# The opening of a two-block kernel: tensor-engine work in a written order, row tiles loaded ahead of weights, modulation sums in blocks of eight, six PSUM banks

## The chip, the cores and the metric

The kernel runs on one core of a Trainium2 chip. The metric is the time of one execution on the device, in microseconds (us). The engines are named by their columns in the profile: PE is the tensor engine (TensorE), PEld its weight loads, DVE is VectorE, ACT is ScalarE, POOL is GpSimd, SP is SyncE, which here issues the DMAs.

## The reference, cut to what matters

Two model blocks run one after the other on 512 rows of 1024 features, all in fp32. The first block has two layers of a mixer and an MLP. The part that matters is the beginning of layer 0:

```python
c_act = silu(c)                                     # one vector of 1024
mod = c_act @ w_ada[0] + b_ada[0]                   # 1024 x 6144, split in six
sh_mix, sc_mix, ... = split(mod, 6)
h = rms_norm(x, g_pre_mix) * (1 + sc_mix) + sh_mix  # 512 x 1024
u = h @ w_in                                        # 1024 x 4096
x_m, z, glu_a, glu_b = split(u, [1024, 2048, 3072])
x_c = silu(causal_depthwise_conv(x_m, 4 taps))      # -> q, k ; x_m -> v
a = glu_a * sigmoid(glu_b)
a = silu(group_layer_norm(causal_depthwise_conv(a, 31 taps)))
y = concat([sigmoid(z) * h_m, a]) @ w_out           # h_m: the mLSTM of q, k, v
x = x + gt_mix * rms_norm(y, g_post_mix)
```

So nothing of `u` can be computed before `sh_mix` and `sc_mix` are there, and these need 2048 columns of `w_ada`, 8 MB.

## The kernel before, in words

**Products.** Each fp32 operand is split into a high part in fp32r and a low part (the rest). A product is three matmuls, high by high, high by low and low by high: `mm3`, lines 163 to 166. ScalarE makes the high part by a cast, and the low part is a subtraction (`sub`, line 143) on VectorE or on GpSimd (argument `P`). Weights pass through three raw buffers (`wrp`), four buffers of high parts (`whp`) and four of low parts (`wlp`). Larger SBUF tiles come from a list of 35 slots (`A`, `free`).

**PSUM.** There are eight banks of 128x512: four for main products (`mm`), two long banks (`long_bank`) in which the 31 taps of the depthwise convolution are accumulated by VectorE, and two for transposes (`tr`).

**The opening.** It has four stages, p = 0 to 3, one for each pair of 128-feature tiles. `stage(p)` (line 1295) runs `ada_first(p)` (line 428): eight loads of 256 KB of `w_ada`, and one matmul for each of the eight contraction tiles, 128x512 with the vector `c` replicated to 32 columns, in four column groups of the array (`tile_position=(0, 32 * g)`, line 439). Their sums lie in a long bank. ScalarE copies them (line 444), TensorE transposes them (line 447), and VectorE reduces and adds (lines 449, 450) and scales (line 391). Then `stage` loads 512 columns of `w_in` (two of the gated unit's column blocks), casts and subtracts them, and `mix[0].turn` transposes the normalised rows (line 218), applies scale and shift on ScalarE (line 224) and splits the result on VectorE (lines 231 and 143). In stage 0 the first two row tiles are loaded between the first loads of `w_ada`, the other two behind them; `post(t)` normalises a row tile (`xnorm`, `row_rstd`: lines 195 to 205). `proj_start` (line 258) holds four banks and, once the next stage has been written down, adds this stage's share to each: 24 matmuls a stage, 96 in all. Its consumer, `glu_cons(0)`, gates the result and starts `taps(0)`.

**After the opening.** Three further groups of the gated unit (`projA`, 96 matmuls each), then four projections of x (`xproj(h)`, 48 matmuls each, with the consumer `xm_cons`: a copy, a split and a convolution of four taps, which read the PSUM bank), q, k and v, the gates, z, the mLSTM, the convolution groups' norms (`conv_norm`, `conv_gate`, `conv_split`), and the projection by `w_out` (`projB_chunk`, and `projB_tail`, whose last two contraction tiles are those of the last convolution group).

**What sets the order.** SyncE's instructions are issued in the order in which the program writes them (`tc.manual_schedule(engines={SP})`). For the other engines a planner fixes the order when the kernel is built: it takes, engine by engine, what by its own cost model is ready, the earliest written first; `tc.high_priority(offset=-LOWP)` sets the taps 4000 places behind. Each engine then works through its own list in that order. Background work (`pending`, for example `ada_pair`) advances by one step with each weight unit that `wunit` loads.

## Time and profile before

Three runs took 2287.65, 2289.1 and 2289.36 us; the median is 2289.1.

| | before |
|---|---|
| profiled execution | 2287.21 us |
| its span, first to last instruction | 2285.2 us |
| PE busy | 98% of the span |
| DVE busy | 67% |
| ACT busy | 43% |
| POOL busy | 13% |
| DMA, mean over the span | 122 GB/s |
| mean granted clock of PE | 0.994 of 2.4 GHz |

A share of busy time is a mean over stages with different limits, so the stretches are read one by one. A matmul's listed duration overlaps the next one's; the pace is the distance from start to start.

### The profile page before, as it was taken

What the parts mean: (1) busy time and instruction counts of PE and PEld (TensorE: products, weight loads), DVE (VectorE), ACT (ScalarE), POOL (GpSimd) and SP (SyncE); (2) the same over time, 40 slices, a digit from 0 to 9 for tenths busy, and PEclk for the clock granted to TensorE, in tenths of its full rate; (3) what the DMA queues carried; (4) which work ended last, traced back from release to release, by engine and by line L of the source; (5) the groups of instructions that cost most, each with busy time, mean ns of one, the idle gap of its engine ahead of it and who ended that gap; (6) DMA issues with size and microseconds to landing.
All of it is one profiled execution on the core that took longest, in us unless ns stands there. A gap on an engine that the chain in (4) does not pass through costs nothing.

```text
span 2285.2 us, 29859 instructions
## 1 busy us (share of the span) xinstructions
PE 2240.0 (98%) x11164; PEld 1807.5 (79%) x11164; DVE 1530.7 (67%) x3037; ACT 979.1 (43%) x1651; POOL 301.3 (13%) x263
## 2 busy tenths in 40 slices
PE   8999999999999999999999999999999999999998
PEld 3777677878777888767887778888888888878886
DVE  4898998874555678899887643387566574652345
ACT  3557554543323334666543332235545554222232
POOL 1763000000000144400000000000321311000000
PEclk9999999999999999999999999999999999999999
DMA  7632134366565232321436544523211321532331
GB/s 265 211 116 79 55 120 131 128 198 194 179 190 176 87 117 85 92 65 47 148 120 187 177 127 127 170 75 114 88 50 54 98 77 60 172 95 94 99 131 65
DMA packets 194585, 277.69 MB, mean 122 GB/s; under 512 B 13812, under 2 KB 146548, under 8 KB 194440
## 3 DMA queue, kind: packets, MB, share of 16 engines
q1 hardware_dynamic: 194440, 275.78, 37.8%
q8 instruction: 88, 1.44, 0.3%
q14 instruction: 57, 0.47, 0.1%
HBM read 263.68 MB, written 14.37 MB: 122 GB/s over the span
## 4 chain that ended last, share of the span: by engine, by line
PE 74%; DVE 5%; ACT 2%; issue 1%; DMA 0%; POOL 0%; SPq 0%; DVEq 0%; ACTq 0%; POOLq 0%
PE mm L166 22%; PE mm L165 22%; PE mm L164 22%; PE cv L1129 1%; PE tr L1114 1%; PE mm L827 1%; PE mm L851 1%; PE mm L1093 0%; PE mm L1095 0%; DVE h L143 0%; PE tr L218 0%; DVE nt L176 0%; ACT sb L1103 0%; DVE h L231 0%; ACT junk L195 0%
## 5 line engine op out<-in xcount | busy, mean ns | idle before, releaser
L164 PE MATMUL mm<-h,wh 128*128 128x512 f32 (+1 forms) x1728 | 656.8, 381 | 3.8 <-DVE h L231 2.9
L165 PE MATMUL mm<-h,wh 128*128 128x512 f32 (+1 forms) x1728 | 654.3, 379 | 0.7 <-DVE h L143 0.6
L166 PE MATMUL mm<-h,wl 128*128 128x512 f32 (+1 forms) x1728 | 654.4, 379 | 0.1
L155 ACT CAST wh<-wr 128x1024 fp32r<-128x1024 f32 (+1 forms) x318 | 323.3, 1018 | 532.4 <-PE mm L165 249.7
L143 DVE TENSOR_TENSOR wl<-wr,wh 128x1024 fp32r<-128x1024 f32 x254 | 314.0, 1240 | 224.4 <-ACT wh L155 223.4
L164 PEld LDWEIGHTS mm<-h,wh 128*128 128x128 f32 x1728 | 324.7, 188 | 75.2 <-DVE h L231 6.8
L166 PEld LDWEIGHTS mm<-h,wl 128*128 128x128 f32 x1728 | 324.8, 188 | 68.3 <-issue 5.9
L165 PEld LDWEIGHTS mm<-h,wh 128*128 128x128 f32 x1728 | 325.3, 188 | 66.1 <-issue 3.0
L589 DVE SCALAR_TENSOR_TENSOR cv<-glu,vec,cv 128x511 f32<-128x511 f32 (+24 forms) x480 | 327.8, 732 | 7.1 <-ACT cv L584 6.8
L362 DVE SCALAR_TENSOR_TENSOR acc<-wr,csil,acc 128x1024 f32<-128x1024 f32 x91 | 116.1, 1284 | 127.6 <-DMA wr<-in_w_ada_dram 88.4
L165 PE MATMUL mm<-wl,hid 128*128 128x512 f32 x416 | 164.2, 395 | 0.0
L166 PE MATMUL mm<-wh,hid 128*128 128x512 f32 x416 | 164.1, 395 | 0.0
L164 PE MATMUL mm<-wh,hid 128*128 128x512 f32 x416 | 163.4, 395 | 0.0
L143 POOL TENSOR_TENSOR wl<-wr,wh 128x1024 fp32r<-128x1024 f32 (+1 forms) x68 | 137.8, 2033 | 185.0 <-ACT wh L155 144.4
L413 POOL PARTITION_BROADCAST G<-row x5 | 8.3, 1665 | 699.5 <-DVE row L410 383.4
L164 PEld LDWEIGHTS mm<-wh,hid 128*128 128x128 f32 x416 | 78.2, 188 | 19.9 <-issue 0.8
L166 PEld LDWEIGHTS mm<-wh,hid 128*128 128x128 f32 x416 | 78.2, 188 | 18.4
L165 PEld LDWEIGHTS mm<-wl,hid 128*128 128x128 f32 x416 | 78.2, 188 | 18.2
L543 ACT ACTIVATE s<-mm 128x512 f32<-128x512 f32 x64 | 38.0, 594 | 111.3 <-PE mm L166 111.3
L1103 ACT ACTIVATE sb<-sb,nm 128x512 f32<-128x512 f32 x64 | 46.4, 725 | 59.1 <-DVE nm L1101 50.2
L1083 POOL TENSOR_TENSOR bias<-band,amask 128x256 f32<-128x256 f32 x48 | 43.3, 910 | 206.5 <-DVE mx L1098 131.1
L546 DVE CAST hid<-s 128x512 fp32r<-128x512 f32 x64 | 29.0, 457 | 45.9 <-ACT s L544 45.9
(318 smaller groups left out, 3659.4 us busy)
## 6 DMA issues: line engine op xcount, KB each, us to landing
wr<-in_w_in_dram SPq DMA_DIRECT2D x140, 512.0 KB
wr<-in_w_ff_dram SPq DMA_DIRECT2D x128, 512.0 KB
wr<-in_w_ada_dram SPq DMA_DIRECT2D x80, 512.0 KB
wr<-in_w_out_dram SPq DMA_DIRECT2D x32, 512.0 KB
wr<-in_w_mod_dram SPq DMA_DIRECT2D x24, 512.0 KB
wr<-in_w_ada_dram SPq DMA_DIRECT2D x32, 256.0 KB
xd<-x SPq DMA_DIRECT2D x16, 512.0 KB
x<-xd SPq DMA_DIRECT2D x16, 512.0 KB
```

The lines of the kernel that those rows point to most:

```text
L143: (eng or V).tensor_tensor(dst, x_, h.bitcast(F32), op=ALU.subtract)
L155: S.copy(h, raw)
L164: PE.matmul(ps, ah, bh, start=first, stop=False)
L165: PE.matmul(ps, ah, bl, start=False, stop=False)
L166: PE.matmul(ps, al, bh, start=False, stop=last)
L362: V.scalar_tensor_tensor(acc, raw, cv[:, kt:kt + 1], acc, op0=ALU.mult, op1=ALU.add)
L543: act(s, ps[m], AF.Relu)
L546: V.tensor_copy(o[:, 0], s)
L589: V.scalar_tensor_tensor(pa[m][:, s:], at[:, m, :512 - s], vv("wdw", l * 248 + (2 * g + m) * 31 + j, 1), pa[m][:, s:], op0=ALU.mult, op1=A ...
L827: PE.matmul(ps[:, :n], k[h][:, kt, j * 128:j * 128 + 128], q[h][:, kt, j * 128:], start=kt == 0, stop=kt == 1)
L1083: P.tensor_tensor(btile[:, b].rearrange("p (c r) -> p c r", r=8), bands[i][:, hh, :, o:o + 32].rearrange("p r c -> p c r"), amask[:, var, ...
L1103: act(sb, sb, AF.Exp, bias=nm, accum_out=sm)
```

## The change

- In `stage(0)` all four row tiles are loaded first, then the weights.
- `ada_first` is cut in three: `ada_load` (eight loads), `ada_sums` (the eight matmuls, one behind the other, in a transposing bank instead of a long bank, and the copy) and `ada_cols` (the rest).
- A stage also loads 256 columns of `w_in` for the first projection of x (half a unit), in a raw buffer of its own, and casts and subtracts it. `stage` is now a generator in four steps: loads; sums; columns, casts and subtractions; transposes of the rows.
- `proj_start` holds six banks, the four main ones and the two long ones, and adds 36 matmuls a stage. Within it TensorE's order is the written one: this stage's banks 0 to 2, the next stage's sums, bank 3, its columns, bank 4, its row transposes, bank 5.
- Its consumers are `glu_cons(0)` and then `xm_cons(0)`; `xproj(0)` is left out of layer 0's later list.
- The second part of the vector table is loaded in stage 1 ahead of that stage's casts.

```diff
-    def proj_start(stage, hT, consumer):
-
-        ps = [mm() for _ in range(4)]
-        cur = stage(0)
-        for p in range(4):
-            if p < 3:
-                nxt = stage(p + 1)
-            h, lo = cur
-            for i in range(4):
-                for k in range(2):
-                    kt, w = 2 * p + k, 2 * (i // 2) + k
-                    c = slice((i % 2) * 128, (i % 2) * 128 + 128)
-                    mm3(ps[i], h[:, w, c], lo[:, w, c], hT[kt][:, 0], hT[kt][:, 1], kt == 0, kt == 7)
-            cur = nxt
-        consumer(ps)
+    def proj_start(lead, hT, consumers):
+
+
+        ps = [mm() for _ in range(4)] + [long_bank() for _ in range(2)]
+        with tc.manual_schedule(engines={mybir.EngineType.PE}):
+            cur = lead(0)
+            for _ in range(4):
+                w = next(cur)
+            for p in range(4):
+                nxt = lead(p + 1) if p < 3 else None
+                if nxt:
+                    next(nxt)
+                for i in range(6):
+                    h, lo = w[i // 4]
+                    for k in range(2):
+                        kt, q = 2 * p + k, 2 * ((i % 4) // 2) + k
+                        c = slice((i % 2) * 128, (i % 2) * 128 + 128)
+                        mm3(ps[i], h[:, q, c], lo[:, q, c], hT[kt][:, 0], hT[kt][:, 1], kt == 0, kt == 7)
+                    if nxt and i in (2, 3, 4):
+                        w_next = next(nxt)
+                if nxt:
+                    w = w_next
+        for k, f in enumerate(consumers):
+            f(ps[4 * k:4 * k + 4])
...
-    def ada_first(p):
-
-
-        ps = long_bank()
+    def ada_load(p):
         wv = wada[0][:, :, 0:2048].rearrange("p k (g n) -> p k g n", g=2)[:, :, :, p * 256:p * 256 + 256]
+        raws = []
         for kt in range(0, 8, 2):
             raw = A([128, 2, 2, 256], F32, "wr")
             for k in range(2):
                 SP.dma_start(raw[:, k], wv[:, kt + k])
-            for k in range(2):
-                g = (kt + k) % 4
-                PE.matmul(ps[32 * g:32 * g + 32, :], crep[:, kt + k], raw[:, k].rearrange("p g n -> p (g n)"),
-                          start=kt < 4, stop=kt >= 4, tile_position=(0, 32 * g))
-            free(raw)
-            yield
+            raws.append(raw)
+        return raws
+
+    def ada_sums(raws):
+
+
+        ps = tr()
+        for kt in range(8):
+            g = kt % 4
+            PE.matmul(ps[32 * g:32 * g + 32, :], crep[:, kt], raws[kt // 2][:, kt % 2].rearrange("p g n -> p (g n)"),
+                      start=kt < 4, stop=kt >= 4, tile_position=(0, 32 * g))
+        free(*raws)
         rows = t2([128, 512], F32, "rows")
         S.copy(rows, ps)
+        return rows
+
+    def ada_cols(p, rows):
         ps = tr()
...
         if l == 0:
-            proj_start(units, hT, glu_cons(0))
+            proj_start(units, hT, (glu_cons(0), xm_cons(0)))
...
-        xproj(0)
+        if l > 0:
+            xproj(0)
         xproj(1)
...
     def stage(p):
 
-        lead = ada_first(p)
         if p == 0:
-            for t in range(2):
-                next(lead)
-                load_x(t)
+            load_x(0, 1, 2, 3)
+        raws = ada_load(p)
+        w = []
+        for cols in ((2048, 3072), (0,)):
+            raw = wrp.tile([128, 2 * len(cols), 256], F32, tag="wr", name="wr")
+            for i, c0 in enumerate(cols):
+                SP.dma_start(raw[:, 2 * i:2 * i + 2], wi_[0][:, 2 * p:2 * p + 2, c0:c0 + 256])
+            w.append(raw)
+        if p == 1:
+            SP.dma_start(vec[:, NLEAD:], I["vec"][:, NLEAD:])
+        if p == 0:
+            for t in range(4):
                 mix[0].post(t)
-        for _ in lead:
-            pass
-        if p == 0:
-            for t in range(2, 4):
-                load_x(t)
-                mix[0].post(t)
-        raw = wrp.tile([128, 4, 256], F32, tag="wr", name="wr")
-        for i, c0 in enumerate((2048, 3072)):
-            SP.dma_start(raw[:, 2 * i:2 * i + 2], wi_[0][:, 2 * p:2 * p + 2, c0:c0 + 256])
-        h = whp.tile([128, 4, 256], F32R, tag="wh", name="wh")
-        lo = wlp.tile([128, 4, 256], F32R, tag="wl", name="wl")
-        S.copy(h, raw)
-        sub(lo, raw, h, P)
+        yield
+        rows = ada_sums(raws)
+        yield
+        ada_cols(p, rows)
+        for u, raw in enumerate(w):
+            n = raw.shape[1]
+            h = whp.tile([128, n, 256], F32R, tag="wh", name="wh")
+            lo = wlp.tile([128, n, 256], F32R, tag="wl", name="wl")
+            S.copy(h, raw)
+            sub(lo, raw, h, P)
+            w[u] = h, lo
+        yield
         for half in range(2):
             mix[0].turn(half, (p,))
...
-        return h, lo
+        yield w
```

## Rows read from the trace of the kernel before

**Rows 1.** The page's engine table: busy us, share of the span, instructions.

```profile
PE 2240.0 (98%) x11164; PEld 1807.5 (79%) x11164; DVE 1530.7 (67%) x3037; ACT 979.1 (43%) x1651; POOL 301.3 (13%) x263
```

**Rows 2.** Windows by stage: stretch, its length, busy us, clock, DMA share, GB/s.

```profile
core 0: us, PE busy (x) PEld busy (x) DVE busy (x) ACT busy (x) POOL busy (x), PEclk, DMA share, GB/s
0.00:26.68 26.68, 15.71 (x41) 3.43 (x41) 14.49 (x60) 10.09 (x24) 3.19 (x8) 0.87 0.97 329
67.49:367.87 300.38, 295.94 (x1332) 230.44 (x1331) 279.78 (x568) 167.29 (x293) 99.93 (x68) 0.99 0.38 122
```

**Rows 3.** Timeline of PE in the opening: start, us, instruction [idle before <-releaser].

```profile
26.68 1.22 PE L164 MATMUL mm<-h,wh 128*128 128x512 f32 x2
...
37.66 1.06 PE L439 MATMUL cv<-wr,crep 128*32 128x512 f32 x8
...
39.62 1.05 PE L439 MATMUL cv<-wr,crep 128*32 128x512 f32 x4
...
41.51 1.05 PE L439 MATMUL cv<-wr,crep 128*32 128x512 f32 x2
...
45.39 0.60 PE L447 MATMUL tr<-ident,rows 128*128 128x128 f32 x4
...
46.67 0.47 PE L164 MATMUL mm<-h,wh 128*128 128x512 f32 x1
...
49.63 1.91 PE L439 MATMUL cv<-wr,crep 128*32 128x512 f32 x12
...
61.35 0.51 PE L164 MATMUL mm<-h,wh 128*128 128x512 f32 x1 [0.31 <-DVE h L231]
...
62.36 0.40 PE L166 MATMUL mm<-h,wl 128*128 128x512 f32 x1
...
67.49 0.39 PE L164 MATMUL mm<-h,wh 128*128 128x512 f32 x1
```

**Rows 4.** Windows of 10 us through the opening.

```profile
0.00:10.00 10.00, 5.11 (x8) 0.73 (x8) 1.95 (x13) 2.84 (x6) 0.82 (x7) 1.00 0.78 250
10.00:20.00 10.00, 6.21 (x26) 2.01 (x25) 7.72 (x31) 6.23 (x16) 1.47 (x1) 0.99 1.08 382
20.00:30.00 10.00, 7.71 (x18) 2.04 (x13) 5.15 (x18) 1.02 (x2) 0.90 (x1) 0.50 1.09 361
30.00:40.00 10.00, 9.97 (x47) 5.67 (x48) 5.79 (x19) 3.46 (x6) 2.39 (x1) 1.00 1.10 368
```

**Rows 5.** Timeline of ACT, DVE and POOL in stages 0 and 3.

```profile
14.02 0.58 ACT L444 COPY rows<-cv 128x512 f32<-128x512 f32 x1 [2.56 <-PE cv L439]
...
15.62 0.16 DVE L450 TENSOR_TENSOR mf<-mf,vec 128x4 f32<-128x4 f32 x1
...
55.15 0.59 ACT L444 COPY rows<-cv 128x512 f32<-128x512 f32 x1 [4.38 <-PE cv L439]
...
56.76 2.40 POOL L143 TENSOR_TENSOR wl<-wr,wh 128x1024 fp32r<-128x1024 f32 x1 [8.25 <-ACT wh L1314]
56.86 2.32 DVE L450 TENSOR_TENSOR mf<-mf,vec 128x4 f32<-128x4 f32 x1
```

**Rows 6.** DVE: groups by line from 62 to 368 us, then the first taps.

```profile
L589 DVE SCALAR_TENSOR_TENSOR cv<-glu,vec,cv 128x511 f32<-128x511 f32 (+24 forms) x240 | 164.3, 732 | 3.8 <-ACT cv L584 3.6
...
L636 DVE SCALAR_TENSOR_TENSOR cv<-mm,vec,cv 128x511 f32<-128x511 f32 (+2 forms) x24 | 17.9, 745 | 0.2 <-ACT cv L633 0.2
...
69.18 7.04 DVE L589 SCALAR_TENSOR_TENSOR cv<-glu,vec,cv 128x511 f32<-128x511 f32 x10
```

**Rows 7.** Timeline of DVE: two of its waits in layer 0's mixer.

```profile
109.95 0.69 DVE L602 SCALAR_TENSOR_TENSOR glu<-th,mm 128x512 f32<-128x512 f32 x1 [2.24 <-ACT th L601]
...
192.49 0.49 DVE L700 BATCH_NORM_STATS2 bs<-cacc 128x6 f32<-128x128 f32 x2 [2.63 <-ACT cacc L697]
```

**Rows 8.** PE at the mixer's closing projection: timeline, then a window.

```profile
389.85 0.79 PE L164 MATMUL mm<-wha,cg 128*128 128x512 f32 x1 [2.11 <-ACT cg L730]
...
390.00:392.00 2.00, 2.00 (x5) 1.23 (x6) 1.97 (x4) 0.81 (x2) 0.00 (x0) 0.50 0.00 0
```

More of the change, by code (lines that the diff above doesn't have):

```diff
@@ L605, in glu_cons @@
             return f
-        if l == 0:
-            proj_start(units, hT, glu_cons(0))
-        else:
-            proj_first(units, hT, lambda: pre.turn(1), glu_cons(0))
-        for g in range(1, 4):
-            projA(wi, [2048 + 256 * g, 3072 + 256 * g], hT, glu_cons(g), eng=None if l == 0 and g == 2 else P)
-        free(glu[0])
-        if l == 0:
-            load_const()
-            free(crep)
         q, k, vf, v1, tz, xmh, xch = {}, {}, {}, {}, {}, {}, {}
-        wg = A([128, 4, 6, 32], F32, "wg")
-        SP.dma_start(wg, I["wg"][l])
         def xm_cons(h):
@@ L645, in xm_cons @@
             return fn
+        if l == 0:
+            proj_start(units, hT, (glu_cons(0), xm_cons(0)))
+        else:
+            proj_first(units, hT, lambda: pre.turn(1), glu_cons(0))
+        for g in range(1, 4):
+            projA(wi, [2048 + 256 * g, 3072 + 256 * g], hT, glu_cons(g), eng=None if l == 0 and g == 2 else P)
+        free(glu[0])
+        if l == 0:
+            load_const()
+            free(crep)
+        wg = A([128, 4, 6, 32], F32, "wg")
+        SP.dma_start(wg, I["wg"][l])
         def xproj(h):
@@ L1318, in stage @@
         if p == 1:
-            SP.dma_start(vec[:, NLEAD:], I["vec"][:, NLEAD:])
             for nm in ("wcm", "bcm", "gmh", "wdw", "gcn", "bcn", "wc2", "bc2"):
                 V.tensor_scalar(vv(nm), vv(nm), 0.5, None, op0=ALU.mult)
-        return h, lo
+        yield w
     mix[0].hT = [HL(512, f"h{f}") for f in range(8)]
```

## The prediction, as recorded before the changed kernel was run

> **What bounds the kernel now.** I read the page's engine table first: TensorE is busy for 2240.0 of 2285.2 us [rows 1], so a change pays only where TensorE waits, runs at the lower clock, or does the same sums in more time. The windows by stage then show where that is. In the first 26.68 us it has only 15.71 us of work, while the DMA engines are full at 329 GB/s [rows 2]; from 67.49 to 367.87 it has 295.94 of 300.38. The third view is its timeline through the opening [rows 3]. The first of the 96 main products (24 in each of four stages) starts at 26.68 and the next group of the projection starts at 67.49. The fourth is granted clock and DMA rate in steps of 10 us [rows 4]: clock 0.50 (the 1.2 GHz level) from 20 to 30, after gaps in TensorE's work, then full.
>
> A second bound lies behind the first. From 67.49 to 367.87 VectorE is busy for 279.78 of 300.38 us [rows 2], mostly with the 240 depthwise-convolution taps of this layer, 0.73 us each [rows 6]. At 389.85 TensorE waits 2.11 us for the last convolution group's output [rows 8]. The end of that chain, not only TensorE, decides when layer 0's mixer ends. So I reckon two sums: TensorE's lead at the end of the opening, and what VectorE's chain lets through.
>
> **Start of the main products.** All four row tiles now load ahead of the modulation weights. From the rates of [rows 4], 2.50 MB have landed by 10 us, 6.32 by 20, 9.93 by 30. Before, the last weights of the first sum stood behind 3.23 MB (0.08 of vectors, 2.10 of weights, 1.05 of rows), at 11.9 us, and the copy of its result began at 14.02 [rows 5], 2.1 later. Now they stand behind 4.28 MB: 14.7 us, copy at 16.8. In return nothing waits for rows afterwards: their 2.18 MB are in by 8.7 us. From copy to first main product I take the last stage's chain, 55.15 to 61.35, 6.2 us [rows 3, 5]: start at 23.0 instead of 26.68. That chain holds a stall. VectorE's small add on line 450 took 0.16 us at 15.62, but 2.32 at 56.86, ending with GpSimd's subtraction, which ran 2.40 from 56.76 [rows 5]. Without it the chain is 4.0 us and the start 20.8. The change adds a half-size subtraction per stage, 1.2 us by half of that row; if it stalls VectorE once more the chain is 7.4 and the start 24.2. I take 23.0, the chain as measured.
>
> The Trainium skill (SBUF — State Buffer, section "SBUF: two separate sides") says that VectorE's instruction with two SBUF inputs and GpSimd's share a port pair under an exclusive lock, held for the whole instruction, so that the loser is blocked. The trace agrees: the add ends 0.02 us after the subtraction. By that rule the second subtraction may block once more, and the end of the opening would come 4.8 us later than without it; by the measured row alone it would not.
>
> **Length of the opening.** Main products pace at 0.233 us: 22 of them from 62.36 to 67.49 [rows 3]. There are now 144 (six banks of 24) instead of 96: 33.6 us. The modulation sums of stages 1 to 3 lie between them. Before, stage 2 took four pieces, and the trace counts two records per matmul: four matmuls together in 1.06 us at 37.66, two in 1.05 at 39.62, then a single one in 1.05 at 41.51 and another like it [rows 3]. One costs what four abreast cost, so 4.2 us a stage. Eight in a row should take two groups, 2.0 us (six took 1.91 at 49.63 [rows 3]; bounds 1.9 and 2.2); three stages 6.0. The 4 and 8 transposes per stage run from 45.39 to 46.67, 1.28 us [rows 3], three times 3.8.
>
> Handover: the next stage's products wait for the 6.2 us chain behind the sums, and TensorE's fixed order has 18 products (4.2) and the transposes (1.3) to cover it: 0.7 us of stall, three times 2.1. Bounds: none with the 4.0 chain, 1.9 each (5.7) with the 7.4 chain. Clock: TensorE is again sparsely fed before its start, so I expect the lower level there; with its lead about 5 us of products at half pace, a loss of 2.6 (bounds 0 and 5, half of the 10 us in [rows 4]). End of opening: 23.0 + 33.6 + 6.0 + 3.8 + 2.1 + 2.6 = 71.1; bounds 64 and 78. The same work before ends at 67.49 plus the 48 products of the first x projection, 11.2: 78.7. **TensorE's lead is 7.6 us.**
>
> **What is free, and behind what.** SyncE's queue is in written order: vectors, four row tiles, then per stage eight weight halves and three loads of projection weights, the rest of the vectors in stage 1. There are three raw buffers and now two are taken per stage, so a load can wait for GpSimd's subtraction of the stage before, with the next stage's modulation weights queued behind it. The last of these stand behind 13.3 MB, 39 us at [rows 4]; they are wanted after two stages, near 49, so 10 us cover the wait; beyond that each us costs one. The casts and subtractions for x (ScalarE, GpSimd) are moved, not added. Two background steps that went with the moved units come two units later, well ahead of their use. The sums move from the two long banks to the transposing banks, each of which is read out within the stage.
>
> **VectorE's chain.** The long banks now hold x's sums, so the first taps (69.18 before [rows 6]) wait until six scalar-tensor operations of x have read them. This is an order, not a cost: x's 7.2 us (six of 0.75 [rows 6], four of about 0.69) stood later. What counts is when VectorE's steady work begins. The gated unit was ready 1.7 us after the fourth bank (67.49 to 69.18); the fourth bank now ends 12 products ahead of 71.1, at 68.3, so 70.0, and 0.4 until x's first copy is there: 70.4, which is 1.2 later than before. Of its 20.6 us of waits [rows 2] those for TensorE's pace go when TensorE leads: 2.24 at 109.95 and 2.63 at 192.49 [rows 7] stand for these, 4.9 in all (bounds 0 and 8). So the convolution's end comes 4.9 - 1.2 = **3.7 us earlier**, and TensorE waits for it with the other 3.9 us of its lead. I forecast 3.7: against the profiled execution's 2287.2 us (2285.2 of span and 2.0 around it) 2283.5. The median of the runs shown, 2289.1, is 1.9 above that execution, so 2285.4 on the clock of the runs.
>
> **Rivals.**
> All of the lead arrives: while the last group is late, TensorE does other sums of the closing projection. For it: the second half of the same row tile and the first sums of the next one don't need that group. Against it: in the trace it stood idle for 2.11 us with such sums still ahead in its program [rows 8], and VectorE's work after 389.85 hangs on the same chain. It gives 2289.1 - 7.6 = 2281.5.
>
> Nothing arrives: VectorE's waits are ScalarE's delays and stay, so only the 1.2 later start is left, with a shorter wait at 389.85 against it: 2289 to 2290. For it: the releaser named in [rows 7] is ScalarE; against it: ScalarE there evacuates what TensorE has just finished.
>
> Slower, by the banks handed to x: if the opening ends late, the taps start late, and VectorE has little slack to regain it. It decides from an opening that ends at 74.8 (where the later start eats the 4.9). With both subtractions blocking and 5 us of clock loss: 24.2 + 33.6 + 6.0 + 3.8 + 5.7 + 5.0 = 78.3, steady work 8.4 later than before, 3.5 after the waits, and up to 2.3 more where TensorE, idle for longer, comes back at half clock, as it did at 390 [rows 8]: 2292.6 to 2295.
>
> That the eight sums would not run abreast is hardly open: four took 1.06 us where one took 1.05 [rows 3].
>
> **How the numbers follow.** Forecast (part of the lead arrives, 2 to 6 us) 0.40; all of it 0.27; nothing 0.16; slower 0.17. The time is the forecast's, 2285.4. A measurement of this kernel tells 0.2%, 4.6 us, from no change: faster means under 2284.5, slower over 2293.7. Faster is the second case and a third of the forecast, 0.41; same the rest of it and nearly all of the third, 0.42; slower 0.17. The likeliest case by itself spans 2283 to 2287; the range for 8 in 10 takes in a full lead with a start at 20.8 (10 us) and most of the slower case: 2279 to 2294.
>
> **What would show it.** In the changed profile: the copy of the first sum at about 16.8 and the first main product near 23; eight sums in one stretch of 2.0 us; the third-stage handover with under 2 us of idle; the next group's first product at about 71 with x's sums done; the first tap at about 77; and at the end of the mixer a wait of TensorE for the last convolution group longer than 2.11 us. The forecast is wrong if that wait is gone (the lead arrived), if the opening ends after 75, or if time changes in stages that the change doesn't touch, since the planner orders all engines but two anew.

## The result, and the profile after

The changed kernel is slower: 2314.33 us (median of 4 runs, 2313.15 to 2318.74) against 2289.23 (4 runs), a ratio of 1.0112 with a 95% interval of 1.0094 to 1.0129. The profiled execution took 2314.08 us with a span of 2312.4, 27.2 more than the span before. The forecast of 2285.4 was wrong, and its range of 2279 to 2294 too.

The engine table of the page comes first, to be set beside [rows 1]: TensorE is busy for 2.2 us less in a span that is 27.2 longer. The time went into waiting, not into work.

```profile
PE 2237.8 (97%) x11164; PEld 1812.1 (78%) x11164; DVE 1530.3 (66%) x3037; ACT 981.6 (42%) x1653; POOL 301.1 (13%) x265
```

The windows that answer to [rows 2] and [rows 4] follow: the lead-in, the opening's 144 products with the modulation sums, then steps of 10 us (stretch, length, busy us of PE, PEld, DVE, ACT and POOL, granted clock, DMA share, GB/s).

```profile
0.00:23.03 23.03, 7.20 (x28) 2.67 (x28) 12.83 (x57) 10.81 (x25) 4.41 (x9) 0.98 0.97 326
23.03:81.79 58.76, 50.72 (x228) 35.31 (x229) 22.60 (x47) 21.60 (x32) 24.69 (x12) 0.86 0.59 202
...
50.00:60.00 10.00, 9.71 (x50) 6.06 (x49) 2.18 (x9) 4.24 (x7) 3.73 (x2) 1.00 0.48 163
60.00:70.00 10.00, 2.91 (x17) 2.15 (x15) 8.01 (x4) 5.27 (x8) 9.40 (x4) 0.82 0.48 166
70.00:80.00 10.00, 9.62 (x29) 7.41 (x30) 2.31 (x6) 2.75 (x4) 2.55 (x2) 0.67 0.25 93
```

Until 60 us all goes nearly as forecast. From 60 to 70 TensorE does 2.91 us of work while GpSimd is busy for 9.40. In the next stretch the mean granted clock is 0.67, between its two levels: 1.2 GHz first, 2.4 GHz at the end. The timeline of TensorE (start, duration, instruction, then in brackets its idle time and what ended it) answers to [rows 3] and [rows 8]:

```profile
23.03 0.79 PE L164 MATMUL mm<-h,wh 128*128 128x512 f32 x1 [4.00 <-DVE h L231]
...
55.26 1.92 PE L453 MATMUL tr<-wr,crep 128*32 128x512 f32 x16
...
70.38 0.80 PE L164 MATMUL mm<-h,wh 128*128 128x512 f32 x1 [7.47 <-DVE h L231]
...
294.35 1.12 PE L712 MATMUL tr<-ident,cacc 128*128 128x128 f32 x4 [11.79 <-ACT cacc L609]
...
394.51 0.60 PE L712 MATMUL tr<-ident,cacc 128*128 128x128 f32 x4
...
415.33 0.80 PE L164 MATMUL mm<-wha,cg 128*128 128x512 f32 x1 [2.11 <-ACT cg L746]
```

There are two long waits: 7.47 us at the last handover (from one stage's products to the next stage's), and 11.79 us at 294 for the third group of the convolution. The wait for the last group's output is 2.11 us as before, but at 415.33 instead of 389.85. After it little differs: 1897.0 us to the end of the span against 1895.4. So the loss, 25.5 us, lies before that point.

In the kernel before, TensorE comes to the transposes of the third and of the last group (the first step of their norm) without a wait:

```profile
270.30 0.60 PE L696 MATMUL tr<-ident,cacc 128*128 128x128 f32 x4
...
369.28 0.60 PE L696 MATMUL tr<-ident,cacc 128*128 128x128 f32 x4
```

From the one to the other it takes 99.0 us, and 100.2 in the changed kernel. So 24.1 of the 25.5 us are lost by the third group's transposes: 11.8 in the wait there, and 12.3 by which TensorE would have come late without it, the last handover among them.

The timelines of GpSimd and VectorE at the last handover and up to the first tap (L605; a tap is L589 in the kernel before) answer to [rows 5] and [rows 6]:

```profile
60.60 2.39 POOL L367 TENSOR_TENSOR acc<-acc,wr 128x1024 f32<-128x1024 f32 x1 [5.35 <-ACT wr L365]
62.95 4.88 POOL L143 TENSOR_TENSOR wl<-wr,wh 128x1024 fp32r<-128x1024 f32 x2
67.79 2.38 POOL L367 TENSOR_TENSOR acc<-acc,wr 128x1024 f32<-128x1024 f32 x1
```

```profile
61.96 1.18 DVE L231 CAST h<-hx 128x256 fp32r<-128x256 f32 x1 [2.13 <-ACT hx L224]
63.17 2.46 DVE L143 TENSOR_TENSOR h<-hx,h 128x256 fp32r<-128x256 f32 x1
65.56 4.77 DVE L231 CAST h<-hx 128x256 fp32r<-128x256 f32 x2
...
70.92 0.28 DVE L231 CAST h<-hx 128x256 fp32r<-128x256 f32 x1
71.23 0.43 DVE L143 TENSOR_TENSOR h<-hx,h 128x256 fp32r<-128x256 f32 x1
...
82.10 1.29 DVE L143 TENSOR_TENSOR xmh<-cv,xmh 128x512 fp32r<-128x512 f32 x2 [0.83 <-ACT xmh L630]
84.24 2.32 DVE L638 SCALAR_TENSOR_TENSOR cv<-cv,vec 128x511 f32<-128x511 f32 x3 [0.86 <-ACT cv L635]
89.79 2.54 DVE L642 SCALAR_TENSOR_TENSOR cv<-th,cv 128x512 f32<-128x512 f32 x1 [3.23 <-ACT th L641]
...
92.92 0.74 DVE L605 SCALAR_TENSOR_TENSOR cv<-glu,vec,cv 128x511 f32<-128x511 f32 x1
...
389.73 3.24 DVE L605 SCALAR_TENSOR_TENSOR cv<-glu,vec,cv 128x484 f32<-128x484 f32 x5
```

GpSimd runs without a gap from 60.60 to 70.17 (subtractions of the next group's weights, and the background step that accumulates the MLP's modulation). In that time VectorE's split of the last rows, 0.28 and 0.43 us apiece when GpSimd is idle (70.92, 71.23), takes 1.18, 2.46 and 2.4 each. The first tap comes at 92.92 instead of 69.18, the last ends at 392.97 instead of 367.86.

The last view is VectorE between its first and last tap, one window for each kernel (the kernel before, then the changed one; stretch, length and columns as above):

```profile
69.18:367.86 298.68, 294.25 (x1325) 229.04 (x1324) 278.93 (x567) 165.60 (x290) 98.24 (x68) 0.99 0.37 120
```

```profile
92.92:392.97 300.05, 279.38 (x1234) 215.30 (x1233) 269.02 (x560) 156.03 (x279) 77.55 (x59) 0.95 0.33 105
```

So the end of the taps is 25.1 us later: the first tap 23.7 later, VectorE's work between 9.9 less (x's first part lies ahead of it now), its idle time 11.3 more (19.75 to 31.03).

### The profile page after: what moved, and what is told of

The parts are those of the page before. It is cut to its first block, busy times and chain, and to the rows that moved or that the text cites. A ratio compares the mean times of both kernels' runs of the same rounds, so it can differ in the third digit from the quotient of the medians.

```text
span 2312.4 us, 29864 instructions
## 1 busy us (share of the span) xinstructions
PE 2237.8 (97%) x11164; PEld 1812.1 (78%) x11164; DVE 1530.3 (66%) x3037; ACT 981.6 (42%) x1653; POOL 301.1 (13%) x265
## 4 chain that ended last, share of the span: by engine, by line
PE 72%; DVE 5%; ACT 2%; DMA 1%; issue 1%; POOL 0%; SPq 0%; DVEq 0%; ACTq 0%; POOLq 0%
PE mm L164 22%; PE mm L166 22%; PE mm L165 22%; PE cv L1146 1%; PE tr L1131 1%; PE mm L844 1%; PE mm L868 1%; DMA wr<-in_w_ada_dram 1%; PE mm L1110 0%; PE mm L1112 0%; DVE h L143 0%; PE tr L218 0%; DVE nt L176 0%; ACT sb L1120 0%; DVE h L231 0%
## 5 line engine op out<-in xcount | busy, mean ns | idle before, releaser
L164 PE MATMUL mm<-h,wh 128*128 128x512 f32 (+1 forms) x1712 | 654.5, 383 | 19.6 <-DVE h L231 14.1
L164 PEld LDWEIGHTS mm<-h,wh 128*128 128x128 f32 x1712 | 322.8, 189 | 90.6 <-DVE h L231 16.8
L605 DVE SCALAR_TENSOR_TENSOR cv<-glu,vec,cv 128x511 f32<-128x511 f32 (+18 forms) x480 | 326.1, 735 | 5.6 <-ACT cv L600 5.5
L164 PEld LDWEIGHTS mm<-wh,hid 128*128 128x128 f32 x416 | 78.2, 188 | 20.3 <-ACT y L538 0.8
L562 DVE CAST hid<-s 128x512 fp32r<-128x512 f32 x64 | 28.1, 441 | 44.5 <-ACT s L560 44.4
```

Of the source, the lines that this page charges most:

```text
L164: PE.matmul(ps, ah, bh, start=first, stop=False)
L562: V.tensor_copy(o[:, 0], s)
L605: V.scalar_tensor_tensor(pa[m][:, s:], at[:, m, :512 - s], vv("wdw", l * 248 + (2 * g + m) * 31 + j, 1), pa[m][:, s:], op0=ALU.mult, op1=A ...
```

## The experiments

Each median is set beside runs of the kernel before on the same chip. In the table, "busy" and "idle" are VectorE's, between its first and last tap. The last four columns come from one profiled execution of each kernel, which took within 2.5 us of the median, but 4.1 more in number 7 and 4.7 less in number 15.

| kernel | us | ratio to before | first tap | busy | idle | last tap ends |
|---|---|---|---|---|---|---|
| before | 2289.2 | 1 | 69.2 | 278.9 | 19.8 | 367.9 |
| changed | 2314.3 | 1.0112 [1.0094, 1.0129] | 92.9 | 269.0 | 31.0 | 393.0 |
| 1 handover cleared | 2310.3 | 1.0090 [1.0075, 1.0105] | 81.7 | 274.0 | 34.9 | 390.5 |
| 2 four banks | 2282.1 | 0.9967 [0.9954, 0.9980] | 67.8 | 274.3 | 20.4 | 362.6 |
| 3 six banks, planner's order | 2309.4 | 1.0082 [1.0065, 1.0099] | 86.3 | 270.8 | 28.3 | 385.4 |
| 4 before, rows first | 2288.3 | 0.9999 [0.9989, 1.0008] | 74.7 | 278.2 | 16.7 | 369.6 |
| 5 four banks, x next | 2284.7 | 0.9987 [0.9978, 0.9996] | 69.2 | 277.7 | 16.2 | 363.1 |
| 6 x copied out | 2317.1 | 1.0129 [1.0113, 1.0146] | 88.5 | 274.5 | 30.4 | 393.4 |
| 7 x read first | 2308.5 | 1.0093 [1.0074, 1.0112] | 96.6 | 266.8 | 21.7 | 385.0 |
| 8 four banks, cleared | 2292.6 | 1.0020 [1.0010, 1.0029] | 67.3 | 275.7 | 26.8 | 369.7 |
| 9 changed, late background | 2322.8 | 1.0155 [1.0138, 1.0172] | 82.1 | 273.4 | 43.6 | 399.1 |
| 10 before, late background | 2306.2 | 1.0079 [1.0064, 1.0094] | 73.2 | 275.7 | 32.9 | 381.8 |
| 11 four banks, late background | 2302.9 | 1.0064 [1.0049, 1.0079] | 70.9 | 275.6 | 33.6 | 380.1 |
| 12 x next, in the long banks | 2319.7 | 1.0137 [1.0122, 1.0152] | 69.2 | 261.6 | 34.6 | 365.4 |
| 13 before, no background | 2295.9 | 1.0028 [1.0017, 1.0039] | 78.4 | 273.1 | 21.4 | 372.9 |
| 14 changed, no background | 2302.3 | 1.0052 [1.0035, 1.0069] | 81.3 | 270.6 | 28.1 | 379.9 |
| 15 x kept for later | 2313.3 | 1.0103 [1.0088, 1.0119] | 75.5 | 280.4 | 32.5 | 388.4 |
| 16 four banks, planner's order | 2287.2 | 0.9995 [0.9986, 1.0005] | 71.7 | 274.7 | 20.7 | 367.2 |
| 17 changed, ScalarE's part early | 2307.1 | 1.0088 [1.0071, 1.0105] | 88.8 | 271.9 | 24.4 | 385.1 |
| 18 four banks, ScalarE's part early | 2283.7 | 0.9977 [0.9968, 0.9986] | 66.6 | 275.8 | 17.6 | 360.0 |

In all rows but number 12 the time less the last column is 1918.7 to 1924.9 us, over last columns from 360 to 399. So the time goes with the end of VectorE's taps to within some 6 us, and each experiment is read by what it does to the three columns that make up that end. That VectorE's last taps hold TensorE up is not shown: in none of these rows does TensorE wait for the last group's transposes (0.0 us), and its wait for that group's output is 2.11 us in every one. Its longest waits for the taps, 9.6 to 12.3 us, are at the third group. Each edit also makes the planner write new lists for all engines that it orders, so no run changes one thing alone.

**1. The last handover cleared.** The next group's subtractions go to VectorE, and the background step starts one group later, so GpSimd has nothing to do there.

```diff
-            projA(wi, [2048 + 256 * g, 3072 + 256 * g], hT, glu_cons(g), eng=None if l == 0 and g == 2 else P)
+            projA(wi, [2048 + 256 * g, 3072 + 256 * g], hT, glu_cons(g), eng=None if l == 0 and g in (1, 2) else P)
+            if l == 0 and g == 1:
+                pending.append(ada_pair(l, 3, "gpl", True))
```

> The changed kernel, but the second group's weight subtractions run on VectorE and the background sums start one group later, so that GpSimd has nothing to do while VectorE makes the last stage's splits. Theory A (GpSimd's work blocks VectorE at the last handover, and that lateness is what the taps inherit): the idle 7.47 us before the last stage falls under 1.5, the half clock behind it goes, the opening ends at 72 to 74 instead of 81.8, and the kernel takes 2299 to 2306. Theory B (the two long banks lent to x delay the taps, whatever the handover): the opening ends earlier, but the kernel stays within 4 us of 2314.

The first product after the handover (TensorE) and the first instruction of GpSimd in 20 us:

```profile
63.57 0.49 PE L164 MATMUL mm<-h,wh 128*128 128x512 f32 x1 [0.36 <-DVE h L231]
```

```profile
78.10 2.41 POOL L367 TENSOR_TENSOR acc<-acc,wr 128x1024 f32<-128x1024 f32 x1 [20.34 <-ACT wr L365]
```

The wait is 0.36 us instead of 7.47, the clock stays at 2.4 GHz, the opening ends at 72.5 and the first tap comes 11.3 earlier. GpSimd's share in that stall is shown, as theory A had it. But only 2.5 us arrive at the last tap: busy time rises by 5.0 (subtractions of about 1.2 us each) and idle time by 3.8, so the time, 2310.3, is nearly theory B's. The edit has a price of its own: on four banks (number 8) it makes the kernel 10.5 us slower. So this run doesn't tell what a clear handover is worth by itself.

**2. Four banks.** x's share leaves the opening and goes back to its old place; row loads, sums in eights and the written order stay.

```diff
-        ps = [mm() for _ in range(4)] + [long_bank() for _ in range(2)]
+        ps = [mm() for _ in range(4)]
...
-                for i in range(6):
+                for i in range(4):
...
-                    if nxt and i in (2, 3, 4):
+                    if nxt and i in (0, 1, 2):
...
-            proj_start(units, hT, (glu_cons(0), xm_cons(0)))
+            proj_start(units, hT, (glu_cons(0),))
...
-        if l > 0:
-            xproj(0)
+        xproj(0)
```

> The changed kernel without x's share: four banks, no x columns in the opening, the first x projection back in its place; rows first, sums in blocks of eight and TensorE's written order stay. Theory A: the stall at the last handover may stay or go with GpSimd's list, and without it the opening ends near 60 (the 71.4 of six banks less 11.2), the kernel takes 2280 to 2287. Theory B: the first tap comes within 3 us of the opening's end, the wait of 11.8 us for a convolution group's norm is gone, and the kernel is at or below the time before, 2280 to 2290, even if the handover stalls. Against both would be 2300 or more.

It is the fastest of all: 32 us below the changed kernel, 6.7 below the one before. So x's share in the opening, with all that hangs on it, carries the whole loss, and the rest of the change is a gain. The edit takes away several things at once (x's loads, its products, the loan of the long banks, the early consumer); numbers 5 to 7, 12 and 15 take them apart.

**3 and 4. The written order, and the rows.** In 3 the written order of TensorE is taken off the six banks; in 4 the kernel before gets its four row loads first.

```diff
-        with tc.manual_schedule(engines={mybir.EngineType.PE}):
+        with ExitStack():
```

```diff
-            for t in range(2):
-                next(lead)
-                load_x(t)
-                mix[0].post(t)
+            load_x(0, 1, 2, 3)
+            for t in range(4):
+                mix[0].post(t)
...
```

> The changed kernel with TensorE's order in the opening left to the planner; six banks, rows first stay. If the written order is what costs (third theory: TensorE stands in line where the planner would have filled the wait): the 7.47 us stall is filled and the kernel falls below 2305. Theories A and B: the planner cuts the sums of eight apart as before (about 2 us per stage more), the opening ends no earlier than 80, and the kernel stays at 2310 to 2320.

> The kernel before with one edit: all four row tiles are loaded ahead of the weights. All theories: the first main product comes near 23 to 24 instead of 26.7, the opening ends 1 to 4 us earlier, and the kernel takes 2284 to 2289. A result above 2294 would mean that the load order or a newly planned order alone costs time.

The written order is not what costs: without it the kernel is 5 us faster, but 20 slower than before, with the same wait at the third convolution group (11.76 us). Loading the rows first starts the products 3.9 us earlier (22.81) but by itself doesn't move the time: the stages then wait for each other by 1.2 to 1.5 us, and the first tap comes at 74.7.

**16. Four banks without the written order.** The same one-line edit as in 3, on the four-bank version.

> The four-bank version (2282.1 us, first main product 22.7, first tap 67.8) with TensorE's order in the opening left to the planner again: rows ahead of weights and sums in eights stay. If the written order makes its gain over before: handovers as in the run with rows first alone (1.2 to 1.5 us each), first tap past 70, 2286 to 2290. If sums in eights with rows first make it: first tap 66 to 69, 2280 to 2284.

At 2287.2 it is at its first case: the first tap is back past 70, and 1.9 us are left of the four-bank version's gain of 6.7. So most of that gain needs the written order.

**5 to 7 and 12. x's place and the long banks.** In 5 x's first projection is a unit of its own behind a four-bank opening; in 12 the same accumulates in the long banks. In 6 ScalarE copies the two lent banks to SBUF at once, and x's consumer reads the copy; in 7 x's consumer is written ahead of the gated unit's.

```diff
             proj_start(units, hT, (glu_cons(0),))
+            projA(wi, [0], hT, xm_cons(0), eng=P)                  # 5
+            projA(wi, [0], hT, xm_cons(0), eng=P, bank=long_bank)  # 12
...
+                if l == 0 and h == 0:                              # 6
+                    xs = A([128, 2, 512], F32, "xs")
+                    for m in range(2):
+                        S.copy(xs[:, m], ps[m])
+                    ps = [xs[:, 0], xs[:, 1]]
...
-        for k, f in enumerate(consumers):                          # 7
+        for k, f in reversed(list(enumerate(consumers))):
```

> The four-bank version (2282.1 us, first tap 67.8, no wait at a convolution norm, first cg at 385.1), but with x's first projection as a unit of its own right behind the opening, through the main banks; x's consumer is again written ahead of three groups of the gated unit, and no long bank is lent. Theory 'the lent banks': the taps still start near 68 to 70, VectorE's chain ends as in the four-bank version give or take 3 us, TensorE has no wait over 3 us at a convolution norm: 2280 to 2287. Rival 'x's consumer moved ahead' (the planner's lists with x's six scalar-tensor operations and ScalarE's part of it early): the third group of taps ends 15 us or more later than 265.7, an 8 to 12 us wait at the third convolution norm: 2300 to 2312. Between the two (2288 to 2299): both have a share.

> The changed kernel, with one addition: ScalarE copies x's two long banks to SBUF at once (two copies of about 0.7 us) and x's consumer reads the copies. So the long banks come free right behind the opening, not behind x's six scalar-tensor operations. The stall of the last handover stays (opening ends near 81.8). Theory 'the lent banks': first tap 85 to 87 instead of 92.9, the chain 6 to 8 us earlier: 2305 to 2309; should the whole loss hang on the banks, 2295 or below. Rival 'x's consumer moved ahead': first tap earlier, but the third group of taps still ends past 288 and the wait at the third convolution norm stays above 8 us: 2310 to 2317.

> The changed kernel with its two consumers written in the other order, x's ahead of the gated unit's. Theory 'the lent banks': the planner now puts x's reads first, the banks come free sooner, first tap near 86 to 90 and the time 2 to 6 us lower: 2308 to 2312. Rival 'x's consumer moved ahead': the same work in the same place, so within 3 us of the changed kernel's 2314, whichever way.

> The version with four banks in the opening and x's first projection as the next unit (2284.7 us, first tap 69.2, last tap ends at 363.1), with one edit: x's first projection accumulates in the two long banks instead of two main banks. So this is the loan alone, without six banks in the opening. In all kernels measured so far the time is the end of the last tap plus 1919 to 1924 us. Theory 'the loan delays the first tap and VectorE's chain keeps the delay': x's products end near 77, first tap at 84 to 90, last tap 375 to 390, time 2296 to 2311. Rival 'the six-bank opening itself, not the loan': VectorE takes x's work, 7 us, first and regains the rest: last tap within 5 us of 363, 2282 to 2290.

Number 5 came out at 2284.7: x's consumer may well stand ahead of three groups, so its early place by itself is not the cost. Number 6 came out as its rival had it, but for the last 0.1 us of its range: the wait for the third group is 11.78 us. The taps' first values (ScalarE's write of tap 31 and the bias into a long bank, with which a group starts) were there at 83.4, right behind the banks' copies, yet the first tap came at 88.5, behind x's splits and convolution in VectorE's list, and the last tap did not move. So it is not only the bank that holds the taps up. Number 7 traded a later first tap (TensorE stood for 13.84 us behind the opening, until ScalarE had read the gate's main banks) for an idle time of 21.7, and gained 5.9 us. Number 12 tested the mirror image: with x's products written behind the gate, the taps took the long banks first and x's products waited for them.

```profile
117.57 0.79 PE L164 MATMUL cv<-h,wh 128*128 128x512 f32 x1 [22.82 <-ACT cacc L609]
...
138.17 0.79 PE L164 MATMUL mm<-h,wh 128*128 128x512 f32 x1 [7.73 <-ACT th L617]
```

These 30 us are TensorE's own and leave the last tap in its place, which is why its row breaks the rule of the table: the taps' end is not the only thing that can set the time. At 2319.7 it is outside both expectations and doesn't settle what a loan ahead of the taps costs.

**8. Four banks with the edit of 1.**

> The four-bank version with the next group's subtractions on VectorE and the background step one group later, which took the 7.5 us stall out of the changed kernel's last handover. The four-bank version has 2.8 us of idle there, with GpSimd busy. If that idle is GpSimd's as well, it goes to under 1 us, the opening ends about 2 us earlier (96th product near 62 instead of 64.3); VectorE gets some 5 us of subtractions of 0.3 to 1 us each. By the chain of VectorE the time follows its end: 2279 to 2284. If the subtractions on VectorE delay the taps instead, 2284 to 2288.

The wait at the last handover only went from 2.83 to 2.33: GpSimd is idle there now, but VectorE has two of the subtractions, 2.36 us, ahead of its split. So the run doesn't tell what the 2.83 were. The time rose to 2292.6, outside both expectations: idle 26.8 instead of 20.4, with TensorE waiting 4.41 us at 161 for a convolution of x.

**9 to 11. The background step later.** It starts behind the fourth group of the gated unit instead of with the first, in the changed kernel, the one before and the four-bank version.

> The changed kernel with one edit: the background modulation step for the MLP (ScalarE scales a loaded row, GpSimd accumulates it) starts after the fourth group of the gated unit, not with the first. In the changed kernel ScalarE stands 43.7 us between 60 and 300 us waiting for that step's loads, with the gated unit's and the taps' instructions behind it in its list, and VectorE is idle for 31.0 us between its first and its last tap (before: 19.8). Theory 'background in the lists of ScalarE and GpSimd': the last handover keeps less than 4 us of its 7.5, VectorE's idle falls to some 20, first tap 80 to 87, time 2293 to 2303. Rival 'late first tap alone, by x in the lent banks': idle stays near 30, time 2306 to 2312 from the shorter handover alone.

> Control: the kernel before with the same edit. If the background steps cost VectorE its waits whatever the opening, the time falls here too, by up to 8 us: 2281 to 2286. If they cost only in the changed opening, 2287 to 2291.

> The four-bank version (2282.1 us) with the same edit. Its last handover has 2.8 us of idle, and VectorE 20.4 us between first and last tap. If the background is behind both: handover under 1 us, idle 14 to 18, time 2275 to 2280. If not: 2281 to 2284; if the steps in their new place meet the last group of taps instead, 2284 to 2290.

My theory was that ScalarE, standing behind this step's loads, makes the added idle. These runs don't bear it out: all three are slower, by 8.5, 18 and 21 us, outside every case expected. But the test is a poor one, since the wait only moved: the step's loads now come among those of the x projections (ScalarE stands for 7.24 us behind one at 147 in number 10), and the idle time rises by some 13 us in each.

**13 and 14. The background step left out,** in the kernel before and in the changed one.

```diff
+        if pool:
+            a0, a1 = A([128, 1024], F32, "acc"), A([128, 1024], F32, "acc")
+            for a_ in (a0, a1):
+                P.memset(a_, 0.01)
+                yield
```

> The kernel before without the background modulation step of layer 0's mixer (left out: the 16 loads of its weights, ScalarE's scaling and GpSimd's accumulation; constants stand in for the sums). It is the baseline for the next run. If ScalarE's 30 us of standing behind those loads are what keeps VectorE idle for 19.8 us between first and last tap, idle falls to 8 to 14 and the time to 2276 to 2284. If the idle has other reasons: 16 to 20 and 2285 to 2289.

> The changed kernel without the same background step. Theory 'background in ScalarE's list makes the added idle': idle 31.0 falls to the level of the run before it give or take 3 us, and what is left between the two is first tap minus the x work done ahead of it, with an opening that loses part of its 7.5 us stall: first tap 81 to 88, 5 to 10 us slower than the kernel before without the step. Rival 'the idle comes with the late start': idle stays 8 or more above that of the run before it and the difference 15 to 25 us.

The result lies between the two. Idle is 21.4 and 28.1: the difference (6.7) is smaller than with the step (11.3) but stays, near the rival's 8. The difference in time is 6.4 us, as the theory had it (5 to 10; the rival 15 to 25), where it is 25.1 with the step. So without the step three quarters of the difference are gone, two thirds of that because the changed kernel gains and one third because the one before loses. The changed kernel gains 12 us, with an opening that ends at 74.6 and a first tap 11.7 earlier. The kernel before lost 6.7 instead of gaining, since the next group's subtractions now ran on GpSimd without a gap, 7.45 us from 62.01, across VectorE's last split (TensorE waits 4.32 us there, first tap at 78.4).

**15. x kept for later.** The edit of 1, with x's banks copied out and x's consumer in its old place behind the gated unit.

```diff
+            xs = A([128, 2, 512], F32, "xs")
+            def keep(ps):
+                for m in range(2):
+                    S.copy(xs[:, m], ps[m])
-            proj_start(units, hT, (glu_cons(0), xm_cons(0)))
+            proj_start(units, hT, (glu_cons(0), keep))
...
+            xm_cons(0)([xs[:, 0], xs[:, 1]])
```

> Six banks, with the next group's subtractions on VectorE (as in the run that cleared the last handover, 2310.3 us, first tap 81.7): ScalarE copies x's two long banks to SBUF behind the opening, and x's consumer works from that copy in its old place, behind the groups of the gated unit. So the long banks come free at once and VectorE's list has no x ahead of the taps. Theory 'x's work ahead of the taps delays them': opening ends near 72.5, first tap 74 to 77, 5 to 8 later than before, last tap 370 to 380, time 2292 to 2302. Rival 'the six-bank opening delays them whatever x's consumer does': first tap past 80, 2305 to 2315. The four-bank version stays the fastest in both, since its first tap comes at 67.8.

The first tap came at 75.5, as the theory had it, but the time at 2313.3, as the rival had it (the profiled execution took 2308.6, with a last tap at 388.4, past the theory's 380). Against number 1: first tap 6.2 earlier, busy 6.4 more, idle 2.3 less. So x's reads ahead of the taps are an order and not a cost, and what remains against four banks is a first tap 7.7 later, 6.1 more work (most of it the subtractions of number 1) and 12.1 more idle.

**17 and 18. ScalarE's part of the taps.** What is common to the changed kernel and numbers 1, 3, 6, 9, 14 and 15, all with a wait of 9.6 to 12.3 us for the third group, and not to before and number 2, stands in ScalarE's timeline where the second group of taps ends: the third group's first values come 5 us behind that end before, and 16 to 21 us behind it in these seven. Before, the group ends at 187.5:

```profile
186.47 0.61 ACT L593 COPY cacc<-cv 128x512 f32<-128x512 f32 x1
191.37 0.60 ACT L593 COPY cacc<-cv 128x512 f32<-128x512 f32 x1
...
192.80 0.83 ACT L584 ACTIVATE cv<-glu,vec 128x512 f32<-128x512 f32 x1
```

In the changed kernel it ends at 218.2:

```profile
220.93 0.60 ACT L609 COPY cacc<-cv 128x512 f32<-128x512 f32 x1
...
236.45 0.61 ACT L609 COPY cacc<-cv 128x512 f32<-128x512 f32 x1
236.92 1.52 ACT L600 ACTIVATE cv<-glu,vec 128x512 f32<-128x512 f32 x2
```

```profile
218.20:237.80 19.60, 18.19 (x83) 14.68 (x84) 9.16 (x11) 17.93 (x32) 3.99 (x5) 0.91 0.37 111
```

The second copy and the third group's first values stand 18 us behind the group's end, after 15 us of other work in ScalarE's list (copies of v, q and k, casts of weights). In the 19.6 us of the window ScalarE is busy for 17.93 and VectorE for 9.16. The edit keeps the low priority for VectorE's taps alone.

```diff
-            with low(LOWP):
-                pa = [long_bank() for _ in range(2)]
-                for m in range(2):
-                    f = 2 * g + m
-                    act(pa[m], at[:, m], AF.Identity, ...)
+            pa = [long_bank() for _ in range(2)]
+            for m in range(2):
+                f = 2 * g + m
+                act(pa[m], at[:, m], AF.Identity, ...)
+            with low(LOWP):
                 for j in range(29, -1, -1):
...
-                for m in range(2):
-                    S.copy(acc[:, m], pa[m])
+            for m in range(2):
+                S.copy(acc[:, m], pa[m])
```

> The changed kernel with one edit: the low priority of the taps (4000 places behind) holds for VectorE's taps alone, no longer for ScalarE's part of a group (two first values, two copies at the end). In ScalarE's list the second group's copies and the third group's first values then stand ahead of most of the q, k and v copies of the last head, as before the change. Theory 'added idle by ScalarE's place in the list': the third group starts within 6 us of the second's end instead of 19.6 behind it, VectorE's idle falls from 31.0 to 18 to 24, the last tap ends at 380 to 387, time 2301 to 2308. The late first tap stays. Rival 'idle goes with the late start whatever the list': last tap 390 to 396, time 2311 to 2318.

> The four-bank version (2282.1 us, idle 20.4, last tap ends at 362.6) with the same edit. Its ScalarE list has the third group's first values ahead of the last head already, so by the same theory little is to be had: idle 16 to 21, time 2278 to 2283. If ScalarE's taps work, now earlier in its list, stands in front of copies that TensorE waits for: 2283 to 2288.

Number 17, timelines of ScalarE and TensorE:

```profile
218.28 0.56 ACT L609 COPY cacc<-cv 128x512 f32<-128x512 f32 x1
...
219.27 0.58 ACT L609 COPY cacc<-cv 128x512 f32<-128x512 f32 x1
219.74 1.49 ACT L599 ACTIVATE cv<-glu,vec 128x512 f32<-128x512 f32 x2
```

```profile
286.71 0.66 PE L712 MATMUL tr<-ident,cacc 128*128 128x128 f32 x4 [1.41 <-ACT cacc L609]
```

The third group starts 1.9 us behind the second's end, its wait on TensorE is 1.41 us instead of 11.79, idle falls to 24.4, and the time by 7.2 us. The theory holds, for more than half of the added idle. TensorE's wait shrinks by more than the time does, since it now reaches the third group 2.7 us later for other waits (3.94 us at 129, 5.02 at 222). In the four-bank version, whose list had the right order already, the time is the same within the intervals; at 2283.7 it is in its second case.

## Why the prediction was wrong

**What held.** The copy of the first sum at 16.75 (16.8 predicted), the first main product at 23.03 (23.0), eight sums in 1.92 us (2.0), the first two handovers (some 0.8 us each by the distance from start to start, 0.7 predicted), and the products at half pace behind the start (13 of them, some 2.8 us lost, 2.6 predicted). The start holds the one stall that it was given (VectorE's scaling took 2.20 us from 18.55, while GpSimd subtracted). The size of the two handovers came right by luck: the chain of 6.2 us that was to make them has that stall in it, and there VectorE's three small instructions took 0.16 to 0.17 us each; TensorE waited for the split of the rows alone. By the terms of the sum the last stage's products were due at 71.1 less 36 of 0.233, 62.7; the stage before ended at 62.9.

**Handover, "0.7 us of stall, three times 2.1 ... 1.9 each".** This term failed at its third place: 7.47 us, then 3.0 more at half pace (36 products in 11.4 us instead of 8.4). With them the opening ends at 81.8, not at 71.1. I had bounded the stall by GpSimd's subtractions of each stage's own weights. What came in its place is the next group's subtractions and the background step, which follow each other on GpSimd for 9.6 us just when VectorE splits the last rows; number 1 shows it. In the kernel before, this lay just behind the last split. So TensorE never had the lead of 7.6 us: the same work was done at 78.7 before and at 81.8 after.

**"This is an order, not a cost".** As to x's work it held (numbers 1 and 15: 6.2 us of start against 6.4 of work). But "VectorE's steady work begins ... 70.4" was 82.1, 11.7 late, of which 10.7 are the opening's; and between there and the first tap VectorE stood for 4.2 us, nearly all of it behind ScalarE.

**"Waits ... for TensorE's pace go when TensorE leads", 4.9 regained (bounds 0 and 8).** This is the step that failed by most. Idle between first and last tap went from 19.8 to 31.0 instead of 14.9, so with the 4.2 the step is 20.3 us off. With 11.7 for the start and 3.2 less work in all, that makes 28.8, the distance from the predicted end of the taps (367.9 + 1.2 - 4.9 = 364.2) to 393.0. The waits were not TensorE's pace: number 1 has the lead that the step asks for (the opening ends at 72.5 instead of 78.7), and its idle time is 34.9. A part of what stood in their place (number 17) is a place in ScalarE's list: the planner had put ScalarE's copies and first values of a group, of low priority like the taps, ahead of the last head's copies before the change and behind most of them after it. This tie the prediction never priced, though it named "time changes in stages that the change doesn't touch" as a sign of being wrong.

**"At 389.85 TensorE waits 2.11 us".** I took this wait for the end of VectorE's chain being late. It is 2.11 in every kernel but number 12, with last taps from 360 to 399. So its length says nothing of how late the taps are, and the sign of a wait "longer than 2.11 us" could not have told the cases apart.

**The rivals.** The slower one came true in kind: it decides from an opening that ends at 74.8, and this one ended at 81.8. Its price of 2292.6 to 2295 was some 20 us short. By its own rule an opening that ends at 81.8 gives 2296; most of the rest is the 4.9 that it too let VectorE regain and the 11.3 of added idle, which it did not have. The handover cleared by number 1's edit doesn't bring the forecast back either (2310.3), because idle and work on VectorE take the place of the stall.

**What stays open.** After number 17 idle is still 4.6 above that of before. In the changed kernel a large part of the idle time stands at 153.5, 9.19 us for ScalarE, which itself stood 7.29 behind a load of the background step:

```profile
150.89 1.15 ACT L365 ACTIVATE wr<-wr,csil 128x1024 f32<-128x1024 f32 x1 [7.29 <-DMA wr<-in_w_ada_dram]
```

```profile
153.53 0.69 DVE L618 SCALAR_TENSOR_TENSOR glu<-th,mm 128x512 f32<-128x512 f32 x1 [9.19 <-ACT th L617]
```

The pair 13 and 14 says that without the step a smaller difference remains. The loss can't be split by adding: clearing the handover, keeping x for later and ScalarE's part early weren't tried together, and an edit as small as the background step's place moved the kernel before by 18 us (number 10). The four-bank version stays the best, and number 18 is equal to it.

## What to carry to other kernels

Where one engine's long chain ends last, judge a change of the opening by when that chain's first instruction starts and by that engine's idle time up to its last, not by how early the tensor engine is done: here the time went with the end of the taps, to within 6 us, over 39 us (whether as its cause is not shown for the last group). Work that fills a tensor engine's gaps ahead of that start (48 products of x) bought nothing here; the same opening without it gained 6.7 us. And when a planner writes each engine's list, a change of the opening can turn the order of two items on a third engine 150 us later, so look in its timeline at the places where the long chain passes from one group to the next.

## What the runs showed of the hardware

VectorE's cast with one SBUF input (128x256, fp32 to fp32r) was held up like its subtraction with two: 0.28 us with GpSimd idle, but 1.18 us once and 2.4 us twice while GpSimd ran instructions of 2.4 us back to back, each of VectorE's instructions ending near the end of one of GpSimd's. The prediction weighed two-input instructions only. Number 1 is the control: with GpSimd idle the same casts took 0.28 to 0.30 us. Number 13 shows it once more (2.44 us for one cast). The Trainium skill (SBUF — State Buffer, section "SBUF: two separate sides") names for the exclusive lock of the shared ports VectorE's instructions in a two-port mode beside those with two SBUF inputs. The trace agrees in that a cast with one input is held up; whether this cast runs in such a mode no run here shows.

The wait of 7.47 us on TensorE was followed by 36 products at 0.32 us each on average instead of 0.233. The granted clock was 1.00 from 62 to 66 us, 0.54 from 66 to 70, 0.50 (1.2 GHz) from 70 to 76 and 0.93 from 76 to 80. So this stall cost 3.0 us more than itself.
